# Lookup tables of a state-space layer, built in three portions with a lower place in the order, on VectorE alone

## The chip, the core and the metric

The kernel runs on one core of a Trainium2 chip. The metric is the time of one execution on the device in microseconds (us), lower is better. The engines are called as in the profile: PE is TensorE's matmul, DVE is VectorE, ACT is ScalarE, POOL is GpSimd, SP issues most of the DMAs.

## The reference, cut to what matters

The program is one step of a hybrid encoder over 1072 positions of width 1024: a layer of gated DeltaNet heads (GDN) beside S5 groups, a feed-forward layer (SwiGLU), a layer of forgetting and differential attention, and another feed-forward layer. The change touches only the first. Its S5 part is a diagonal complex state-space model, and the GDN part needs a triangular solve for each block of 64 positions:

```python
def s5_mixer(u, re0, im0, lam_re, lam_im, log_dt, b_re, b_im, c_re, c_im, d_skip, glu_w, glu_b):
    ...
    dt = jnp.exp(log_dt.astype(jnp.float32))[:, None]
    mag = jnp.exp(lr * dt)
    ar, ai = mag * jnp.cos(li * dt), mag * jnp.sin(li * dt)
    ...
    bbr = cr[..., None] * br - ci[..., None] * bi
    bbi = cr[..., None] * bi + ci[..., None] * br
    ...
    _, _, xr, xi = lax.associative_scan(combine, (a_r, a_i, bur, bui), axis=1)
    y = (jnp.einsum('btgp,gmp->btgm', xr, c_re.astype(jnp.float32))
         - jnp.einsum('btgp,gmp->btgm', xi, c_im.astype(jnp.float32))
         + uf * d_skip.astype(jnp.float32).reshape(SSM_GROUPS, SSM_GROUP))

def gated_delta_rule(q, k, v, beta, logg, s0):
    ...
    sol = lax.linalg.triangular_solve(a_low + jnp.eye(CHUNK, dtype=a_low.dtype), rhs,
                                      left_side=True, lower=True)
```

The kernel evaluates the S5 scan by tables that depend on the parameters alone: phases of the powers of the complex pole for 130 steps, and products of the first nine powers with the matrices b and c. These tables are what the change moves.

## The kernel before, in words

Nearly all PE time is dense matmul. The first layer's input projection comes as weight tiles of 128 columns (`dense`): for each tile three chunks of 360, 360 and 352 positions, each of 72 / 3 = 24 matmuls in split precision (`mm3`, L72 to L74). Each chunk fills a PSUM tile `pm`, of which there are two, so PE begins a chunk when the one two before it has been evicted by DVE (L943, a product with the norm `er` into `pre`; 128x360, 128x352 and, for the last chunk split at the group border, 128x32 and 128x328). After the third chunk DVE also makes three convolution steps on the tile (L950, 128x1104) and the low half of the next weights (L38, `wl`).

The 16 tiles of q and k come in three groups of heads (0 to 2, 3 to 5, 6 and 7). After a group's tiles each head has a `pre_head`: decays and products of k and q in PSUM tiles `pk` (L1010, L1011), evicted by DVE (L1014, L1015) into a tile `N`, whose diagonal blocks go to DRAM (L1020, `ndr`). Then `substitute` reads the blocks of the whole group back (L1029, `NB`), inverts them on POOL with 31 pairs of L1037 and L1039, and writes `xdr`. `inverse` then loads the blocks (`iv<-xdr`) and squares its way to the whole inverse on PE, beginning with L1056. Tiles are taken from rings in one pool: `N` and `iv` four each, `ms` and `m2` three each, `gcr` and `TB` two each; a tile's new use waits for the end of its old one. `gcr` is loaded with a head's decays and is last read by POOL's L1017; DVE's first reader of it is L988.

`S5.early` makes the S5 tables. It is a generator: first parameters, then phases (two halves `hh`, table `P`, by doubling, L599 to L609), then for each of four quarters `hf` two complex products with the powers (`ep`, 128x512, and `ca`, 128x576), transposes of `ep` on PE (L631), and a small matmul of `bd` (a `TB` tile) with `ca` (L650) whose result DVE copies out (L652). Every complex product is `cmul` (L406 to L419): four products, one difference, one sum. With `alt=g` two of the four products (L411, L413) run on POOL, the rest on DVE.

The order of instructions on each engine is fixed when the program is built. A scheduler takes instructions by readiness in a model of the engines and, among those, by a priority that follows the order of the code; `next(early)` in the loops over tiles and heads puts the tables' pieces between the pieces of group 0. DMAs of the tables (`s5pd`, `s5ed`, `s5cad`, `hsc`) are issued by SP.

Of the kernel before, what the change touches and what calls it, by code (L numbers as in the profile page):

```python
# [466 lines left out]
SB = {'M': 1, 'D': 4, 'Y': 4, 'ys': 2, 'wU': 2}  # L467
NP = 4


class S5:
# [96 lines left out]
    def early(self, st1, s1t, pkt):  # L568
# [4 lines left out]
        self.params()  # L573
        cc = self.cc
        yield
# [10 lines left out]
        tb = [small("ms", 512, 3) for x in range(3)]  # L586
        cmul(v, bb, [cc[:, x].unsqueeze(2).to_broadcast([128, 16, 16]) for x in range(2)], [mats[:, 0], mats[:, 1]], [m16(x) for x in tb])
        v.tensor_mul(dl, self.dsk.unsqueeze(2).to_broadcast([32, 16, 16]), self.e16.unsqueeze(1).to_broadcast([32, 16, 16]))

        iv = [s1t("iv", 4) for x in range(4)]  # L590
        for hh in range(2):
            ps = slice(8 * hh, 8 * hh + 8)
            P = iv[2 * hh:2 * hh + 2]
            Pv = [x[:, :1088].rearrange("p (a j) -> p a j", a=8) for x in P]
            tv = [x.rearrange("p (a j) -> p a j", a=8) for x in tb]
            v.memset(Pv[0][:, :, 5:6], 1.0)
            v.memset(Pv[1][:, :, 5:6], 0.0)
            for x in range(2):
                v.tensor_copy(Pv[x][:, :, 6:7], self.u8[:, x, ps].unsqueeze(2))  # L599
            n = 1  # L600
            while n < 130:
                m = min(n, 130 - n)
                a = [Pv[x][:, :, 6:6 + m] for x in range(2)]
                b = [Pv[x][:, :, 5 + n:6 + n].to_broadcast([128, 8, m]) for x in range(2)]
                o = [Pv[x][:, :, 6 + n:6 + n + m] for x in range(2)]
                cmul(v, o, a, b, [x[:, :, :m] for x in tv], alt=g if m > 8 else None)
                n += m
                if n == 16:
                    yield  # L609
            for x in range(2):  # L610
                v.tensor_copy(Pv[x][:, :, 0:5], Pv[x][:, :, 5:10])
                for q in range(2):
                    nc.sync.dma_start(self.pd[2 * hh + q, x], P[x][:, 544 * q:544 * q + 544])
            yield
        zero = small("ms", 512, 3)[:16, :112]
        g.memset(zero, 0.0)
        nc.sync.dma_start(self.hsc[:, :, :, 0:112].rearrange("m a e q -> m (a e) q"), zero.unsqueeze(1).to_broadcast([16, 32, 112]))
        t = [iv[0][:, :576], iv[0][:, 576:], iv[1][:, :576]]

        def powers(o, M, ps, nd, neg):  # L620
# [1463 lines left out]
```

## Time and profile before

| | us |
|---|---|
| median of 3 runs | 3350.07 |
| lowest and highest run | 3346.22, 3354.53 |
| the profiled execution | 3354.03 |
| span of its trace | 3352.2 |
| PE busy | 3181.3 (95% of the span) |
| DVE busy | 1909.8 (57%) |
| ACT busy | 1192.7 (36%) |
| POOL busy | 1022.7 (31%) |

The profiled execution took 1.8 us more than its span, and lies 4 us above the median of the runs. Its mean granted clock is 0.969 of full speed. PE is the engine to watch: 3352.2 - 3181.3 = 170.9 us of idle time in all, and where the clock was lower a busy PE does less. The part of the program that the change touches ends about 600 us after the start.

### The profile page before, as it was taken

Reading aid. Unit: us, or ns where it says so; the run is one execution under the profiler, and the core shown is the slowest. Engines: PE = TensorE matmul, PEld = TensorE weight load, DVE = VectorE, ACT = ScalarE, POOL = GpSimd, SP = SyncE. Lnnn points to the kernel's source line nnn. Section 1 sums busy time; section 2 is a strip of 40 time slices with the busy share of each in tenths; the row PEclk is TensorE's granted clock in tenths of the full one; section 3 lists DMA queues with packets and bytes.
Section 4 is the critical chain, followed back from the end, with each engine's and each line's share of the span. In section 5 each row is a group of like instructions: output and inputs, shape, how many; then the busy total and the mean of one; then the engine's idle time right before and its main releaser. Section 6 shows DMA issues by size and latency. Waiting matters only on the chain. (4 is left out here: it accounts for less than half of the span.)

```text
span 3352.2 us, 54659 instructions
## 1 busy us (share of the span) xinstructions
PE 3181.3 (95%) x21673; PEld 3052.7 (91%) x21673; DVE 1909.8 (57%) x3558; ACT 1192.7 (36%) x2221; POOL 1022.7 (31%) x1018
## 2 busy tenths in 40 slices
PE   7899998999989999999999999998998999999997
PEld 6889998998888999999999998876788999999996
DVE  8986554535437655556337225657767655556434
ACT  5434332244434222223114115555655222223112
POOL 2347563412210555541003002223210555551003
PEclk9899999999999999999999999997998999999998
DMA  3454534556432222226113445544424222226211
GB/s 104 157 177 129 167 106 130 160 189 239 162 135 79 77 78 77 78 84 232 52 59 118 162 125 153 158 135 128 139 84 169 77 80 79 78 80 214 74 46 67
DMA packets 167225, 405.24 MB, mean 121 GB/s; under 512 B 42333, under 2 KB 71793, under 8 KB 166969
## 3 DMA queue, kind: packets, MB, share of 16 engines
q1 hardware_dynamic: 142360, 332.86, 31.4%
q10 hardware_dynamic: 16704, 44.33, 3.6%
q0 software_dynamic: 7904, 24.56, 2.1%
q8 instruction: 171, 2.80, 0.3%
q14 instruction: 86, 0.70, 0.1%
HBM read 273.78 MB, written 127.89 MB: 120 GB/s over the span
## 5 line engine op out<-in xcount | busy, mean ns | idle before, releaser
L72 PE MATMUL pm<-mv,wh 128*128 128x352 f32 (+2 forms) x2272 | 752.1, 332 | 28.9 <-DVE pre L943 22.8
L74 PE MATMUL pm<-mv,wl 128*128 128x352 f32 (+2 forms) x2272 | 747.5, 330 | 2.9 <-POOL wl L38 2.3
L73 PE MATMUL pm<-mv,wh 128*128 128x352 f32 (+2 forms) x2272 | 747.9, 329 | 0.0
L72 PEld LDWEIGHTS pm<-mv,wh 128*128 128x128 f32 (+1 forms) x2272 | 429.5, 189 | 38.1 <-issue 15.6
L74 PEld LDWEIGHTS pm<-mv,wl 128*128 128x128 f32 (+1 forms) x2272 | 429.2, 189 | 7.0 <-POOL wl L38 2.9
L73 PEld LDWEIGHTS pm<-mv,wh 128*128 128x128 f32 (+1 forms) x2272 | 429.5, 189 | 3.3 <-issue 0.5
L37 ACT ACTIVATE wh<-wraw 128x512 fp32r<-128x512 f32 (+4 forms) x182 | 148.8, 818 | 702.6 <-PE pm L73 599.6
L255 PE MATMUL pq<-mv,wl 128*128 128x268 f32 x2112 | 295.0, 290 | 8.6 <-DVE xslot L265 3.6
L255 PE MATMUL pq<-mv,wh 128*128 128x268 f32 x2112 | 289.3, 287 | 5.1 <-ACT wh L37 3.2
L255 PEld LDWEIGHTS pq<-mv,wl 128*128 128x128 f32 x2112 | 278.0, 192 | 9.2 <-issue 3.8
L255 PEld LDWEIGHTS pq<-mv,wh 128*128 128x128 f32 x2112 | 272.6, 189 | 6.0 <-ACT wh L37 5.9
L104 POOL TENSOR_TENSOR acc<-acc,sq 128x360 f32<-128x360 f32 (+3 forms) x35 | 35.5, 1013 | 512.1 <-ACT sq L103 511.6
L342 DVE TENSOR_TENSOR xslot<-xslot,pm 128x360 f32<-128x360 f32 x144 | 75.0, 524 | 168.4 <-PE pm L74 168.4
L236 POOL TENSOR_TENSOR sab<-wraw 128x512 f32<-128x512 f32 x20 | 26.2, 1309 | 461.1 <-DMA wraw<-in_w_dram 322.6
L38 DVE TENSOR_TENSOR wl<-wraw,wh 128x512 fp32r<-128x512 f32 (+4 forms) x144 | 135.6, 942 | 45.0 <-ACT wh L37 43.5
L309 POOL TENSOR_TENSOR xslot<-xslot,r 128x1072 f32<-128x1072 f32 x44 | 121.1, 2774 | 0.1
L255 PE MATMUL pq<-us,wl 128*128 128x268 f32 x858 | 119.2, 287 | 0.0
L255 PE MATMUL pq<-us,wh 128*128 128x268 f32 x858 | 118.6, 286 | 0.0
L950 DVE SCALAR_TENSOR_TENSOR cy<-pre,convw,cy 128x1104 f32<-128x1104 f32 x72 | 109.9, 1526 | 14.8 <-ACT cy L948 13.7
L38 DVE TENSOR_TENSOR wh<-sab,wh 128x512 fp32r<-128x512 f32 x88 | 74.3, 846 | 68.2 <-ACT wh L37 68.2
L255 PEld LDWEIGHTS pq<-us,wl 128*128 128x128 f32 x858 | 111.6, 189 | 0.0
L255 PEld LDWEIGHTS pq<-us,wh 128*128 128x128 f32 x858 | 111.0, 188 | 0.0
(765 smaller groups left out, 7073.5 us busy)
## 6 DMA issues: line engine op xcount, KB each, us to landing
ud<-xslot SPq DMA_DIRECT2D x44, 536.0 KB
sab<-ud SPq DMA_DIRECT2D x44, 536.0 KB
wraw<-in_w_dram SPq DMA_DIRECT2D x44, 512.0 KB
xraw<-in_w_dram SPq DMA_DIRECT2D x44, 512.0 KB
wraw<-in_wie_dram SPq DMA_DIRECT2D x36, 512.0 KB
qkvd<-cy ACTq DMA_DIRECT2D x24, 552.0 KB
wraw<-in_wio_dram SPq DMA_DIRECT2D x24, 512.0 KB
kq<-qkvd SPq DMA_DIRECT2D x16, 552.0 KB
```

Source lines behind the costliest of these rows:

```text
L37: nc.scalar.activation(h, src, AF.Copy)
L38: (eng or nc.vector).tensor_sub(l, src, f(h))
L72: nc.tensor.matmul(ps, a, h[:, c0:c1], start=start and k == 0, stop=False)
L73: nc.tensor.matmul(ps, a, l[:, c0:c1], start=False, stop=False)
L74: nc.tensor.matmul(ps, b, h[:, c0:c1], start=False, stop=stop and k == kt - 1)
L104: (eng or nc.gpsimd).tensor_add(acc[:, c0:c1], acc[:, c0:c1], s)
L236: eng.tensor_add(S1, A21, A22)
L255: nc.tensor.matmul(p[:, 512 * j:512 * j + HC], op[:, wo + 128 * k:wo + 128 * k + 128], B[nm][k][:, xo + HC * j:xo + HC * j + HC], start=ne ...
L309: g.tensor_mul(o, o, r)
L342: nc.vector.tensor_add(X[m][:, c0:c1], X[m][:, c0:c1], p)
L950: v.scalar_tensor_tensor(y[:, :TG], pre[:, j:j + TG], convw[:, i, j:j + 1], y[:, :TG], op0=OP.mult, op1=OP.add)
```

## The change

`early` is split. `phasors` (parameters and phases) is written after the `pre_head`s of group 0, and `powers` twice, after those of group 1 (quarters 0 and 1) and of group 2 (quarters 2 and 3). All three stand in `tc.high_priority(offset=-2000)`, which gives their instructions a lower place among those that are ready. `alt=g` is gone from them, so that all six operations of each `cmul` are DVE's. The load of the matrices `mats`, the product `bb` and the term `dl` are made twice, once for each `powers`. In the built program POOL has 27 instructions fewer, DVE 35 more, and PE the same ones in another order.

```diff
+LATER = 2000
...
-    def early(self, st1, s1t, pkt):
+    def phasors(self, st1, s1t):
...
-            P = iv[2 * hh:2 * hh + 2]
+            P = [s1t("iv", 4) for x in range(2)]
...
-                cmul(v, o, a, b, [x[:, :, :m] for x in tv], alt=g if m > 8 else None)
+                cmul(v, o, a, b, [x[:, :, :m] for x in tv])
                 n += m
-                if n == 16:
-                    yield
...
+    def powers(self, st1, s1t, pkt, hfs):
...
+        mats = s1t("N", 4)[:, :1024].rearrange("p (c a b) -> p c a b", c=4, a=16)
+        g.dma_start(mats, I['s5m'])
+        bb = [m16(small("m2", 256, 3)) for x in range(2)]
+        dl = m16(small("m2", 256, 3))[:32]
+        cmul(v, bb, [cc[:, x].unsqueeze(2).to_broadcast([128, 16, 16]) for x in range(2)], [mats[:, 0], mats[:, 1]],
+             [m16(small("ms", 512, 3)) for x in range(3)])
...
-            cmul(v, [f4(x) for x in o], A, B, [f4(x) for x in t], neg_im=neg, alt=g)
-        for hf in range(4):
+            cmul(v, [f4(x) for x in o], A, B, [f4(x) for x in t], neg_im=neg)
+        for hf in hfs:
...
-                N = []
-                for h in range(a, b):
-                    N.append(pre_head(h, nd[h - a]))
-                    next(early, None)
-                    next(early, None)
-                return nd, xd, N
+                return nd, xd, [pre_head(h, nd[h - a]) for h in range(a, b)]
...
                 for h in range(*GR[n]):
-                    for i in (1, 0):
-                        qkv(i, h)
-                        next(early, None)
+                    qkv(1, h)
+                    qkv(0, h)
                 G[n] = group(n)
-                for x in early:
-                    pass
+                with tc.high_priority(offset=-LATER):
+                    if n == 0:
+                        s5.phasors(st1, s1t)
+                    else:
+                        s5.powers(st1, s1t, pkt, (2 * n - 2, 2 * n - 1))
                 group2(n, G[n])
                 group3(n, G[n])
```

The built order shows what this does on the engines (line numbers above 468 are one higher after the change, and 635 to 655 stand for other lines of the tables).

DVE before, inside one dense tile of group 0, some 228 us after the start. The rows with `acc`, `m_744`, `m_745` and `N` are products of the quarters (`N` is here the tile of `mats`, `m_744` and `m_745` are `bb`), between evictions L943 and convolution steps L950:

```order
L943 TENSOR_TENSOR pre<-pm,er 128x360
L950 SCALAR_TENSOR_TENSOR cy<-pre,convw,cy 128x1104
L415 TENSOR_TENSOR iv<-iv 128x512
L414 TENSOR_TENSOR iv<-acc,m_745 128x512
L414 TENSOR_TENSOR iv<-acc,N 128x576
L412 TENSOR_TENSOR iv<-acc,N 128x576
L943 TENSOR_TENSOR pre<-pm,er 128x352
L419 TENSOR_TENSOR iv<-iv 128x512
L38 TENSOR_TENSOR wl<-wraw,wh 128x1024
L415 TENSOR_TENSOR iv<-iv 128x576
L950 SCALAR_TENSOR_TENSOR cy<-pre,convw,cy 128x1104
L417 SCALAR_TENSOR_TENSOR iv<-iv 128x576
```

After the change no such row stands among the tiles of group 0. DVE after, 220 rows later in its order, in the tile that follows the inverses of group 0; the products L411 and L413, which were POOL's, now stand here too:

```order
L944 TENSOR_TENSOR pre<-pm,er 128x352
L419 TENSOR_TENSOR iv<-iv 128x512
L411 TENSOR_TENSOR iv<-acc,N 128x576
L412 TENSOR_TENSOR iv<-acc,N 128x576
L944 TENSOR_TENSOR pre<-pm,er 128x32
L944 TENSOR_TENSOR pre<-pm,er 128x328
L413 TENSOR_TENSOR iv<-acc,N 128x576
L951 SCALAR_TENSOR_TENSOR cy<-pre,convw,cy 128x1104
L414 TENSOR_TENSOR iv<-acc,N 128x576
L415 TENSOR_TENSOR iv<-iv 128x576
L944 TENSOR_TENSOR pre<-pm,er 128x360
```

The quarters 0 and 1 have moved from the tiles of group 0 to the time of its inverses and of the tile after them; quarters 2 and 3 stand in the same way behind the inverses of group 1. The phases stay where they were, among the second to fifth tile.

POOL before, in the middle of the first `substitute`. L1017 is the last reader of the `gcr` of head 2 or 3, and the load of a later head's `gcr` waits for it:

```order
L1039 TENSOR_TENSOR XB<-XB,TB 108x26x6
L1001 COPY egl<-gcr 128x9
L1002 COPY egl<-gcr 128x1
L1037 TENSOR_TENSOR TB<-NB,XB 108x175
L1017 TENSOR_TENSOR gcr<-kq,gcr 128x1104
L1039 TENSOR_TENSOR XB<-XB,TB 108x25x7
```

POOL after, at the beginning of the same `substitute`:

```order
L1018 TENSOR_TENSOR gcr<-kq,gcr 128x1104
L1023 MEMSET N 32x9x32 x4
L1038 TENSOR_TENSOR TB<-NB,XB 108x31
L1040 TENSOR_TENSOR XB<-XB,TB 108x31
L1038 TENSOR_TENSOR TB<-NB,XB 108x60
```

That L1017 (now L1018) has moved ahead of the first step of `substitute`, and no product of the tables is left on POOL around it.

## Rows read from the trace of the kernel before

**Rows 1.** The page, busy time and share of the span, PE alone.

```profile
PE 3181.3 (95%) x21673; PEld 3052.7 (91%) x21673; DVE 1909.8 (57%) x3558; ACT 1192.7 (36%) x2221; POOL 1022.7 (31%) x1018
```

**Rows 2.** Waits of PE, first 900 us: total us, times, longest.

```profile
PE pm L72 <- DVE pre L943: 22.8, 11, 5.1
```

**Rows 3.** Windows of 50 us: PE, PEld, DVE, ACT, POOL busy, granted clock, DMA.

```profile
100.00:150.00 50.00, 39.84 (x232) 38.84 (x232) 48.39 (x150) 26.00 (x27) 21.18 (x33) 0.89 0.35 122
150.00:200.00 50.00, 48.26 (x331) 47.46 (x330) 44.42 (x80) 18.18 (x19) 23.74 (x23) 0.97 0.56 181
200.00:250.00 50.00, 44.84 (x301) 42.82 (x300) 43.95 (x84) 15.59 (x17) 19.25 (x22) 0.97 0.52 167
250.00:300.00 50.00, 44.85 (x273) 43.73 (x272) 33.18 (x71) 23.88 (x24) 41.27 (x63) 0.90 0.38 128
300.00:350.00 50.00, 50.00 (x387) 49.76 (x387) 33.76 (x75) 24.46 (x33) 23.50 (x41) 1.00 0.54 172
350.00:400.00 50.00, 50.00 (x365) 50.00 (x364) 32.01 (x81) 16.36 (x21) 27.50 (x55) 1.00 0.55 174
...
500.00:550.00 50.00, 42.05 (x287) 41.38 (x287) 18.49 (x25) 13.97 (x22) 19.14 (x35) 0.93 0.25 78
```

**Rows 4.** DVE by line and shape, 30 to 420 us: busy us, mean ns.

```profile
L415 DVE TENSOR_TENSOR iv<-iv 128x576 f32<-128x576 f32 x4 | 6.0, 1510 | 4.2 <-PE pk L650 4.2
...
L412 DVE TENSOR_TENSOR iv<-acc,N 128x576 f32<-128x576 f32 x4 | 4.9, 1234 | 0.0
L417 DVE SCALAR_TENSOR_TENSOR iv<-iv 128x576 f32<-128x576 f32 x4 | 4.7, 1174 | 0.0
...
L414 DVE TENSOR_TENSOR iv<-acc,N 128x576 f32<-128x576 f32 x4 | 3.9, 983 | 0.0
...
L412 DVE TENSOR_TENSOR iv<-acc,m 128x512 f32<-128x512 f32 x4 | 2.6, 650 | 0.5 <-DMA s5pd<-iv 0.5
```

**Rows 5.** POOL by line and shape, 30 to 420 us.

```profile
L411 POOL TENSOR_TENSOR iv<-acc,m 128x512 f32<-128x512 f32 x4 | 11.4, 2838 | 12.4 <-DVE iv L415 8.4 <-DMA s5pd<-iv 4.1
```

**Rows 6.** Timeline of DVE: start, us, instruction, wait before it.

```profile
111.72 0.22 DVE L411 TENSOR_TENSOR ms<-iv 128x64 f32<-128x64 f32 x1
...
136.18 1.10 DVE L411 TENSOR_TENSOR ms<-iv 128x64 f32<-128x64 f32 x1
...
278.72 0.51 DVE L988 TENSOR_TENSOR gsm<-gcr,stats 128x9 f32<-128x9 f32 x1 [6.09 <-DMA gcr<-gcd]
```

**Rows 7.** Window of 10 us, columns as in Rows 3.

```profile
280.00:290.00 10.00, 10.00 (x44) 10.00 (x45) 7.24 (x10) 5.15 (x6) 9.48 (x10) 0.55 0.17 54
```

**Rows 8.** Timeline of POOL around the substitutes of groups 0 and 1.

```profile
245.13 0.19 POOL L936 COPY pre<-cstate 128x3 f32<-128x3 f32 x1 [11.43 <-DVE N L1015]
...
259.82 0.24 POOL L1037 TENSOR_TENSOR TB<-NB,XB 108x31 f32<-108x31 f32 x1 [2.96 <-DMA NB<-ndr]
...
268.88 2.56 POOL L1017 TENSOR_TENSOR gcr<-kq,gcr 128x1104 f32<-128x1104 f32 x1
...
311.77 0.25 POOL L1039 TENSOR_TENSOR XB<-XB,TB 108x31 f32<-108x31 f32 x1
374.56 0.24 POOL L1037 TENSOR_TENSOR TB<-NB,XB 108x31 f32<-108x31 f32 x1 [3.51 <-DMA NB<-ndr]
...
419.50 0.25 POOL L1039 TENSOR_TENSOR XB<-XB,TB 108x31 f32<-108x31 f32 x1
```

**Rows 9.** Timeline of PE: a dense stretch, and the first inverse matmul of groups 0, 1, 2.

```profile
317.28 0.32 PE L73 MATMUL pm<-mv,wh 128*128 128x352 f32 x1
317.44 0.32 PE L74 MATMUL pm<-mv,wl 128*128 128x352 f32 x1
...
319.22 0.46 PE L1056 MATMUL gp<-iv,N 128*128 128x128 f32 x2
427.35 0.46 PE L1056 MATMUL gp<-iv,N 128*128 128x128 f32 x2 [1.46 <-DMA iv<-xdr]
523.51 0.77 PE L1056 MATMUL gp<-iv,N 128*128 128x128 f32 x2 [5.61 <-DMA iv<-xdr]
```

More of the change, by code (lines that the diff above doesn't have):

```diff
@@ L566, in params @@
         self.cc = cc
-    def early(self, st1, s1t, pkt):
-        cx, I = self.cx, self.I
-        nc = cx.nc
-        v, g = nc.vector, nc.gpsimd
+    def phasors(self, st1, s1t):
+        nc = self.cx.nc
+        v = nc.vector
         self.params()
-        cc = self.cc
-        yield
-        def small(nm, n, bufs):
-            return st1.tile([128, n], F32, name=nm, bufs=bufs)
-        def m16(x):
-            return x[:, :256].rearrange("p (a b) -> p a b", a=16)
-        mats = s1t("N", 4)[:, :1024].rearrange("p (c a b) -> p c a b", c=4, a=16)
-        g.dma_start(mats, I['s5m'])
-        bb = [m16(small("m2", 256, 3)) for x in range(2)]
-        dl = m16(small("m2", 256, 3))[:32]
[L586 to L590, printed above, removed]
+        tb = [st1.tile([128, 512], F32, name="ms", bufs=3) for x in range(3)]
+        tv = [x.rearrange("p (a j) -> p a j", a=8) for x in tb]
         for hh in range(2):
             ps = slice(8 * hh, 8 * hh + 8)
-            P = iv[2 * hh:2 * hh + 2]
+            P = [s1t("iv", 4) for x in range(2)]
             Pv = [x[:, :1088].rearrange("p (a j) -> p a j", a=8) for x in P]
-            tv = [x.rearrange("p (a j) -> p a j", a=8) for x in tb]
             v.memset(Pv[0][:, :, 5:6], 1.0)
@@ L613, in early, with small, m16, times @@
                     nc.sync.dma_start(self.pd[2 * hh + q, x], P[x][:, 544 * q:544 * q + 544])
[L614 to L617, printed above, removed]
+    def powers(self, st1, s1t, pkt, hfs):
+        cx, I = self.cx, self.I
+        nc = cx.nc
+        v, g = nc.vector, nc.gpsimd
+        cc = self.cc
+        def small(nm, n, bufs):
+            return st1.tile([128, n], F32, name=nm, bufs=bufs)
+        def m16(x):
+            return x[:, :256].rearrange("p (a b) -> p a b", a=16)
+        mats = s1t("N", 4)[:, :1024].rearrange("p (c a b) -> p c a b", c=4, a=16)
[4 more added lines that the diff above has]
+             [m16(small("ms", 512, 3)) for x in range(3)])
+        v.tensor_mul(dl, self.dsk.unsqueeze(2).to_broadcast([32, 16, 16]), self.e16.unsqueeze(1).to_broadcast([32, 16, 16]))
+        if 0 in hfs:
+            zero = small("ms", 512, 3)[:16, :112]
+            g.memset(zero, 0.0)
+            nc.sync.dma_start(self.hsc[:, :, :, 0:112].rearrange("m a e q -> m (a e) q"), zero.unsqueeze(1).to_broadcast([16, 32, 112]))
+        iv = [s1t("iv", 4) for x in range(4)]
         t = [iv[0][:, :576], iv[0][:, 576:], iv[1][:, :576]]
-        def powers(o, M, ps, nd, neg):
+        def times(o, M, ps, nd, neg):
             f4 = lambda x: x[:, :64 * nd].rearrange("p (a d m) -> p a d m", a=4, d=nd)
@@ L623, in powers @@
             B = [M[x][:, ps].unsqueeze(2).to_broadcast([128, 4, nd, 16]) for x in range(2)]
-            cmul(v, [f4(x) for x in o], A, B, [f4(x) for x in t], neg_im=neg, alt=g)
-        for hf in range(4):
+            cmul(v, [f4(x) for x in o], A, B, [f4(x) for x in t], neg_im=neg)
+        for hf in hfs:
             ps = slice(4 * hf, 4 * hf + 4)
             ep = [iv[2][:, :512], iv[2][:, 576:1088]]
-            powers(ep, bb, ps, 8, False)
+            times(ep, bb, ps, 8, False)
             for x in range(2):
@@ L635, in early @@
                 nc.sync.dma_start(self.ed[hf, x], e)
-            yield
             ca = [iv[3][:, :576], iv[3][:, 576:]]
-            powers(ca, [mats[:, 2], mats[:, 3]], ps, 9, True)
+            times(ca, [mats[:, 2], mats[:, 3]], ps, 9, True)
             for x in range(2):
@@ L655, in early @@
                 nc.sync.dma_start(self.hsc[:, ps, e, 112:240], hv[16 * e:16 * e + 16])
-            yield
     def load(self, hf):
```

2 lines of the change are left out of this document (removed).

## The prediction

> **What bounds the kernel now.** The page's busy times come first: PE works for 3181.3 of 3352.2 us [rows 1]. The dense matmuls are all still needed, so the change can only win back time in which PE stands idle or runs at less than the full clock. Next come PE's waits: in the first 900 us the largest entry is the start of a dense chunk that waits for DVE's eviction L943, 22.8 us in eleven waits [rows 2]. DVE as a whole is busy for 57%, but that is a mean; the windows say where it is short. From 100 to 250 us DVE is busy for 48.39, 44.42 and 43.95 of each 50 us, and there PE stands still; from 300 to 400 us PE never stops, and DVE is busy for only 33.76 and 32.01 [rows 3].
>
> I count as lost in a window its idle time and, of its busy time, the share by which the granted clock is below 1. That gives for 100 to 150 us 10.16 + 0.11 x 39.84 = 14.5 us; for 150 to 200 us 1.7 + 1.4 = 3.2; for 200 to 250 us 5.2 + 1.3 = 6.5; for 250 to 300 us 5.15 + 4.5 = 9.6; for 500 to 550 us 7.95 + 2.9 = 10.9 [rows 3]. The clock follows the idle time: after the wait of 5.1 us that ended at 279.8 the next 10 us have PE busy throughout at a granted clock of 0.55, close to the lower level of 1.2 GHz, a loss of another 4.5 us [rows 2, 7]. So a wait costs PE up to twice its length, and a wait saved gives back as much.
>
> **All products on VectorE.** One product of a quarter costs POOL 2.84 us for 128x512 [rows 5]; DVE made a like product, L412 of the same shape, in 0.65 us [rows 4]. Handing DVE six operations in place of four need not make it later. With POOL beside it, the four 128x576 operations of a complex product took 1.23 + 0.98 + 1.51 + 1.17 = 4.9 us [rows 4]. By its width an undisturbed one should take 0.65 x 576 / 512 = 0.73 us, an estimate, so six take 4.4. For 128x512 I charge two more at 0.65, or 1.3. The four quarters thus change by 4 x (1.3 - 0.5) = +3 us; bounds are -2 (no charge for the 128x512) and +6 x 4 (every operation stays at some 1.2 us, the two new ones too). I take +3, because the same DVE operation of 128x64 took 0.22 us with POOL silent and 1.10 us beside POOL's product [rows 6]; the surplus is in the company and not in the shape. The Trainium skill ("SBUF — State Buffer", "Who interferes with whom") says that a VectorE instruction with two inputs in SBUF contends with a GpSimd instruction that reads SBUF. These rows agree, and by it the sum keeps the +3 as long as POOL does not read beside the tables.
>
> The repeated `bb` and `dl` are 7 operations of up to 128x256 at 0.33 us (half of 0.65), 2.3 us on DVE once more. This and the +3 lie in the new places, and are costed there.
>
> **The phases (100 to 160 us).** They stay in the same tiles. DVE gets for each half the two products of 128x128, 128x256 and 128x512, which at 0.65 us for the largest and in proportion are 2 x 1.14 = 2.3 us, 4.6 us for both. It loses the surplus: two rows of 128x64 at about 1.1 us that fall to 0.22, L415 of 128x512 at 1.5 in place of 0.65, and others like them [rows 6], some 5 us. That is nothing, within 2 us. But the first quarter's products, which follow at once, leave these tiles, so that DVE catches up a tile earlier. Of the 14.5 us lost I take 8 as won, the bounds are 0 (DVE is as late as now) and 14.
>
> **The quarters leave group 0 (160 to 300 us).** Here lost time is 3.2 + 6.5 + 9.6 = 19.3 us. All four quarters go from here, at about 8 us of products each (4.9 + 3.1) plus copies, 40 us of DVE's 121 us in 150 to 300. What is left is some 80 of 150 us, as little as in 300 to 400 us, where nothing is lost [rows 3]. The wait of 5.1 us is of another kind: DVE stood for 6.09 us before L988 for the load of `gcr` with the next eviction behind it [rows 6], and that load needed POOL's L1017, which ran only at 268.88, in the middle of `substitute` [rows 8]. In the new order it stands before `substitute`. I take 16 as won, bounds 9 (the `gcr` load or another wait stays) and 19.
>
> **The first inverse.** PE is no longer slowed, but the chain to the inverse is not PE's. In the order after the change, PE's rows between the last product of group 0's heads (L1011) and the first L1056, each at its duration in the trace of before, add up to 55.9 us; in the order of before they are 61.9. The chain beside it: eviction to the reading of the blocks, 245.1 to 259.8 = 14.7 us, `substitute` from 259.8 to 312.0 = 52 us, and 7.2 us to the first inverse matmul at 319.2 [rows 8, 9]. On POOL the second becomes shorter, because the `gcr` product and some evictions' copies are no longer in its midst: its own operations are 41 us, and that of group 1 took 45.2 (374.6 to 419.75) [rows 8]. The table DMAs in front of the block loads leave SP, so the first part is between 8 and 14.7. So the chain is 55 to 68 us, against 55.9: a wait of 0 to 12 us, I take 4, with 2 us more for the clock behind it [rows 7]. Term +6, bounds 0 and +20.
>
> **The quarters beside the inverses.** In 300 to 400 us DVE has 34 us free of 100 [rows 3], and each `powers` brings 2 x (4.4 + 3.9) + 2 x 2 for copies + 2.3 + 1.5 = some 24 us. Over the 81 us of PE work of the inverses and two tiles this fits: 0.66 x 81 + 24 = 78. But it is not spread evenly. Between the evictions of one dense tile (PE about 15 us, 72 matmuls at 0.16 us and small ones [rows 9]) the new order has 19 table rows, 13.5 us at 0.65 to 0.73, beside 0.66 x 15 = 9.9 of other work: 23.4 us of DVE. PE can run two chunks (8 us) ahead of it. Term +3, bounds 0 and +8. Behind group 1 DVE has more free time; nothing.
>
> **Groups 1 and 2.** `substitute` of group 1 and `bd` of the quarters share the two `TB`. Its first step now waits for PE's small matmul of quarter 0; from there to the first inverse matmul PE has 50.4 us, and the chain needs 45.2 or less plus 7.5, 51 to 53, up to 58 if DVE's tables beside it slow POOL. Today's wait is 1.46 us [rows 9]. I take 4 us with 1 us for the clock: term +4, bounds -2 and +12. For group 2 the same count is 58.8 us against about 63; today 5.61 us are waited for and 10.9 lost [rows 3, 9]. Term -2, bounds -10 and +4.
>
> **Sum.** -8 - 16 + 6 + 3 + 4 - 2 = -13 us. The profiled execution of 3354.0 becomes 3341. It lies 4 us above the median of 3350.1, so for a median I say **3337 us**. Later stages change by single rows in their order only, and I give them nothing, with 4 us to either side.
>
> **The rivals.**
> First, *given back*: the waits of the inverses grow as much as the tiles gain. They do so if the chain's part from the heads to the blocks stays 14.7 us and `substitute` stays near 50 us. Then group 0 waits 12 us and loses 5 more at the lower clock, group 1 stands at +8: -24 + 17 + 3 + 8 - 2 = +2, 3352 us. For it speaks that waits of 1.46 and 5.61 us are already there today [rows 9]; against it, that POOL loses all the tables' products. Chance 0.25.
>
> Second, *slower*: the tables' DVE rows delay PE more where they are now than where they were. The place is the tile with 23.4 us of DVE work, and the small matmuls of the quarters in PE's order, which stand in front of dense chunks. It decides if `mats`, which waits for a tile `N` that PE releases only in the second inverse of the group, comes so late that DVE's queue, and with it evictions, stand behind it. With two groups, a stall of 6.1 us as today's for `gcr` [rows 6] in each, and each doubled by the clock, the sum is -13 + 24 = +11 and with tile 15's full 8 us +16: 3366 us. The Trainium skill ("Perfetto Trace Analysis", "Optimizing Scalar/DVE Operations") speaks that way too: it says that with VectorE saturated, moving work to Scalar or even GPSIMD may make sense, and adds that the shared port may keep it from helping. In the phase stage DVE is nearly saturated (48.39 of 50), and the 4.6 us of products would then be a loss [rows 3]. Chance 0.15.
>
> Third, *all won*: neither inverse waits, and nothing is late in the new places: -14 - 19 - 2 = -35, 3315 us. `substitute` would have to follow within 8 us of the heads and run in 41. Chance 0.1.
>
> Fourth, *the phases decide*: the change does not do what it says at its first portion, whose rows stand where they stood. If the 14.5 us of 100 to 150 stay, the sum is -5, 3345 us. Chance 0.1, within the spread of the forecast.
>
> **How the numbers follow.** Forecast 0.4, given back 0.25, slower 0.15, all won 0.1, phases 0.1. A change of 0.3% is 10 us, about what can be told from none: faster is below 3340, slower above 3360. Faster: nearly three quarters of the forecast (0.29), all won (0.1), the part of the phases' case in which the other terms come out better (0.05), and of the first two rivals that in which half of their price stays away (0.09): 0.53. Slower: the second rival and the tail of the first, 0.19. The same: 0.28. The range from 3315 to 3360 leaves out the second rival and a little at the low end.
>
> **What would show it.** Right: the waits L72 <- DVE L943 between 150 and 300 us gone, L988 without a long wait for `gcr`, DVE under 35 of 50 us there, the first inverse matmul well before 319 us, with a wait of 0 to 12 us on its block load, table rows of 128x576 at 0.7 to 0.8 us. Wrong: L411 and L413 on DVE at 1.2 us or more; PE waits of several us for L943 or for the tables' transposes between 300 and 350 us; DVE waiting for `mats`; or the phase stage as slow as it is now.

## The result and the profile after

The changed kernel takes 3374.55 us (median of four runs, 3371.47 to 3380.92); the kernel before, run beside it, 3349.9 (3346.22 to 3354.53). The ratio is 1.0075 [1.0056, 1.0095]: it is slower, by about 25 us. The forecast of 3337 us and its range both missed, and the sign was wrong. The profiled execution took 3380.92 us, 6 us above this median, with a span of 3379.1, 26.9 us more than the span before.

The page's busy times of after, to be read against [rows 1]: PE, the matmuls, has the same count of instructions and is busy 11.8 us longer, and POOL loses 27 us of work. VectorE has 35 instructions more and is busy 4 us less, as its operations became shorter.

```profile
PE 3193.1 (94%) x21673; PEld 3058.2 (91%) x21673; DVE 1905.7 (56%) x3593; ACT 1195.6 (35%) x2221; POOL 996.0 (29%) x991
```

The windows of 50 us, with the columns of [rows 3]:

```profile
100.00:150.00 50.00, 40.37 (x208) 39.10 (x206) 36.13 (x113) 24.85 (x25) 6.42 (x16) 0.80 0.35 113
150.00:200.00 50.00, 49.22 (x333) 49.16 (x333) 33.82 (x83) 19.46 (x19) 6.81 (x19) 0.97 0.44 148
200.00:250.00 50.00, 46.61 (x302) 45.00 (x301) 30.37 (x60) 22.40 (x23) 19.16 (x39) 1.00 0.57 195
250.00:300.00 50.00, 41.90 (x285) 41.70 (x284) 29.60 (x58) 18.44 (x19) 36.10 (x60) 0.90 0.32 95
300.00:350.00 50.00, 46.65 (x373) 45.61 (x372) 36.67 (x109) 18.65 (x33) 13.76 (x25) 1.00 0.64 184
350.00:400.00 50.00, 47.32 (x297) 44.94 (x296) 37.18 (x70) 20.04 (x21) 37.21 (x48) 0.93 0.41 147
...
500.00:550.00 50.00, 45.28 (x274) 43.13 (x273) 23.35 (x29) 13.17 (x12) 47.10 (x69) 1.00 0.23 82
```

Three things stand in them. VectorE has become free where it was short: 36.13, 33.82 and 30.37 us of each 50 between 100 and 250 us, where it had 48.39, 44.42 and 43.95. PE gained next to nothing from it: from 150 to 250 it is busy 2.7 us more, and from 250 to 300 for 41.90 us in place of 44.85. And from 300 to 400 us, where it never stood still before, it now stands 3.35 and 2.68 us, with the clock at 0.93 in the second window.

Lost time, as the prediction counts it, but summed over windows of 10 us, says where the 25 us arise (us lost from the start of the span to the time at the head of the column):

| kernel | 150 | 300 | 450 | 600 | 1000 | 1200 |
|---|---|---|---|---|---|---|
| before | 41.8 | 61.3 | 62.8 | 76.5 | 111.1 | 121.8 |
| after | 44.0 | 60.2 | 74.6 | 91.7 | 130.8 | 140.7 |

Up to 300 us the two are level: nothing was won in the stage whose tiles were to win 24 us. Between 300 and 600 us 16 us are lost more, from there to 1000 some 4 more. The waits of PE in the first 900 us of after (total us, times, longest) name the new places:

```profile
PE gp L1057 <- DMA iv<-xdr: 11.7, 2, 8.7
PE pm L72 <- DVE pre L944: 10.9, 11, 3.1
PE pk L1011 <- DVE N L1016: 10.6, 3, 8.1
PE pm L960 <- ACT pre L956: 8.4, 4, 4.0
PE pm L74 <- POOL wl L38: 4.7, 3, 2.1
```

The waits for the eviction of a dense tile have halved, from 22.8 us [rows 2] to 10.9. In their place have grown the load of the substituted blocks for the inverse (L1057; 7.1 us before), the eviction of a head's matrix (L1016; 2.4 before) and ScalarE's L956, whose result L960 sums (0.3 before).

The wait of 8.1 us has its cause on VectorE. The first two rows are its timeline, the third is PE's:

```profile
286.92 0.27 DVE L645 MEMSET TB<- 128x256 f32 x1 [10.91 <-POOL XB L1040]
287.11 0.23 DVE L1016 SCALAR_TENSOR_TENSOR N<-pk,gsm,N 128x128 f32<-128x128 f32 x1
...
287.39 0.80 PE L1011 MATMUL pk<-kq 128*128 128x128 f32 x2 [8.10 <-DVE N L1016]
```

L645 clears `bd`, the small operand of a quarter. It needs nothing but a free buffer of `TB`, and it stands early in the order, among the evictions of the heads. The buffer is held by the first `substitute` on POOL, which ends at 286.8. So VectorE stands for 10.91 us with the eviction L1016 queued behind the memset, and PE stands behind that.

The same two buffers stop POOL in the other direction, and VectorE once more:

```profile
363.44 3.07 POOL L1038 TENSOR_TENSOR TB<-NB,XB 108x31 f32<-108x31 f32 x1 [10.44 <-PE pk L652]
...
417.89 0.27 DVE L645 MEMSET TB<- 128x256 f32 x1 [9.15 <-POOL XB L1040]
```

The second `substitute` waits for the small matmul L652 of the quarters, and a memset of the next portion for the end of that `substitute`.

The third `substitute` begins at 491.49 us, before at 457.97. Its blocks are not what is late: they are asked for at 456.06, before at 454.69. But its `TB` is held by a quarter of the second portion until that quarter's last L652, and on POOL two products for the weights of dense tiles (L38) stand in front of it in the order. A row of SP, one of PE and two of POOL:

```profile
456.06 0.31 SPq L1030 DMA_DIRECT2D NB<-ndr  x1
...
485.57 1.72 PE L652 MATMUL pk<-iv,TB 128*32 128x128 f32 x14
...
486.71 4.10 POOL L38 TENSOR_TENSOR wl<-wraw,wh 128x1024 fp32r<-128x1024 f32 x1 [6.87 <-ACT wh L37]
...
491.49 0.70 POOL L1038 TENSOR_TENSOR TB<-NB,XB 72x31 f32<-72x31 f32 x1
```

Without a second portion (e13 below) the same `substitute` begins at 461.85, after 2.35 us for its blocks. In after its inverse ends the chain with PE's longest wait here:

```profile
425.27 0.46 PE L1057 MATMUL gp<-iv,N 128*128 128x128 f32 x2 [2.94 <-DMA iv<-xdr]
561.01 0.77 PE L1057 MATMUL gp<-iv,N 128*128 128x128 f32 x2 [8.73 <-DMA iv<-xdr]
```

Against [rows 9] (1.46 and 5.61 us at 427.35 and 523.51) the third group is 37.5 us later.

### The profile page after: what moved, and what is told of

The parts are those of the page before. It is cut to its first block, busy times and chain, and to the rows that moved or that the text cites. A ratio compares the mean times of both kernels' runs of the same rounds, so it can differ in the third digit from the quotient of the medians.

```text
span 3379.1 us, 54664 instructions
## 1 busy us (share of the span) xinstructions
PE 3193.1 (94%) x21673; PEld 3058.2 (91%) x21673; DVE 1905.7 (56%) x3593; ACT 1195.6 (35%) x2221; POOL 996.0 (29%) x991
## 5 line engine op out<-in xcount | busy, mean ns | idle before, releaser
L72 PE MATMUL pm<-mv,wh 128*128 128x352 f32 (+2 forms) x2272 | 752.8, 332 | 17.7 <-DVE pre L944 10.9
L38 DVE TENSOR_TENSOR wl<-wraw,wh 128x512 fp32r<-128x512 f32 (+4 forms) x144 | 134.1, 931 | 41.2 <-ACT wh L37 39.9
L38 DVE TENSOR_TENSOR wh<-sab,wh 128x512 fp32r<-128x512 f32 x88 | 77.2, 878 | 68.0 <-ACT wh L37 68.0
```

The costliest lines, as they stand in the source:

```text
L38: (eng or nc.vector).tensor_sub(l, src, f(h))
L72: nc.tensor.matmul(ps, a, h[:, c0:c1], start=start and k == 0, stop=False)
```

## The experiments

The question to the experiments was which part costs: VectorE alone, the lower place, the shared `TB`, the work of the quarters, or where the portions stand between the groups. Each ratio is to the kernel before, run in the same batch on the same chip; "+7 us" is the ratio less one, times that kernel's 3354 to 3358 us. Every build has its own order on every engine, so one edit also shifts rows far from it. The diffs without another word are against the changed kernel.

### Where it stands, and on which engine

**e1_own_ring**: `bd` gets a buffer of its own; the room comes from `kq` and `gcr`, cut to the width that they use.

```diff
-            bd = small("TB", 256, 2).rearrange("p (x a b) -> p x a b", x=2, a=4)
+            bd = small("bd", 256, 1).rearrange("p (x a b) -> p x a b", x=2, a=4)
...
-                return st1.tile([128, 1152], F32, name=nm, bufs=bufs)
+                return st1.tile([128, TG if nm in ("kq", "gcr") else 1152], F32, name=nm, bufs=bufs)
```

> The changed kernel, but the small tile bd of the quarters has a ring of its own (one buffer) in place of the TB ring that it shares with substitute; so that it fits, the tiles kq and gcr are 1104 columns wide in place of 1152. Theory 1 (the shared ring): the waits of 10.9 and 9.2 us before VectorE's memset of bd, PE's wait of 8.1 us at 287 us with its low clock, and the wait of 10.4 us before the second substitute vanish; 14 to 22 us less than the changed kernel, 3353 to 3360, near the kernel before. Theory 2 (all products on VectorE cost the time) and theory 3 (the place beside the inverses saturates VectorE): within 5 us of the changed kernel, 3370 to 3379.

Measured: 1.0099 [1.0077, 1.0121], +33 us. The wait at L1011 falls to 1.0 us, but the first inverse, at the same time as in after (294.37 against 295.06), now shows the wait itself:

```profile
294.37 0.55 PE L1057 MATMUL gp<-iv,N 128*128 128x128 f32 x1 [8.31 <-DMA iv<-xdr]
```

So the stall at the memset was real and cost nothing of its own up to the first inverse: in its absence PE runs through its work and waits for the same `substitute` 7 us further on. The shared `TB` alone is not the cause.

**e2_pool_back**: the products go back to POOL, in the new places.

```diff
-                cmul(v, o, a, b, [x[:, :, :m] for x in tv])
+                cmul(v, o, a, b, [x[:, :, :m] for x in tv], alt=nc.gpsimd if m > 8 else None)
...
-            cmul(v, [f4(x) for x in o], A, B, [f4(x) for x in t], neg_im=neg)
+            cmul(v, [f4(x) for x in o], A, B, [f4(x) for x in t], neg_im=neg, alt=g)
```

> The changed kernel with two of the four products of each complex product of the tables back on GpSimd (alt=g as before), in the new places. Theory 1: the shared ring still makes VectorE wait, no gain: 3368 to 3390, a surplus on VectorE of 1 us per 128x576 operation beside GpSimd. Theory 2: back near the kernel before, 3350 to 3358.

Measured: 1.0021 [1.0008, 1.0034], +7 us. Its third `substitute` starts at 495.0 and S5's first matmul of the main part stands at 614.7, as late as after's (491.49 and 615.44). From 300 to 600 us it loses 28.5 us, nearly as much as after (31.5; before 15.2). Of the 12 us that its trace has lost less than after's in all, 4 arise up to 300 us and 5 behind 600. So the loss between the groups stays when the products return to POOL, and the 18 us between e2 and after cannot be put down to the engine alone.

**e3_dve_old_place**: the kernel before with VectorE alone, everything in its old place.

```diff
-                cmul(v, o, a, b, [x[:, :, :m] for x in tv], alt=g if m > 8 else None)
+                cmul(v, o, a, b, [x[:, :, :m] for x in tv])
...
-            cmul(v, [f4(x) for x in o], A, B, [f4(x) for x in t], neg_im=neg, alt=g)
+            cmul(v, [f4(x) for x in o], A, B, [f4(x) for x in t], neg_im=neg)
```

> The kernel before with all products of the tables on VectorE, in the old places. Theory 1: as fast as the kernel before or a little faster, 3340 to 3352, since the products that VectorE takes over are paid by the surplus that it loses. Theory 2: as slow as the changed kernel, 3368 to 3380.

Measured: 1.0006 [0.9996, 1.0016], no difference. It has lost 6.5 us less by 300 us (54.8 against 61.3), and gives it back at the first inverse, whose load of the blocks is now waited for:

```profile
325.84 0.77 PE L1056 MATMUL gp<-iv,N 128*128 128x128 f32 x2 [6.32 <-DMA iv<-xdr]
```

**e4_normal_place**: the portions keep their ordinary place in the scheduler's order.

```diff
-LATER = 2000
+LATER = 0
```

> The changed kernel with LATER = 0: the three portions keep their place in the code but no longer have a lower place among ready instructions. Theory 1: the memset of bd still stands before the last evictions of the heads in VectorE's order, so the waits stay: 3368 to 3382. Theory 3 in the form that the lower place delays what PE waits for: 3350 to 3360.

Measured: 1.0063 [1.0043, 1.0083], +21 us. The second `substitute` stands behind L652 for 9.54 us, as in after for 10.44. The lower place alone isn't the cause.

**e7_own_ring_pool_back**: e1 and e2 together (both diffs above).

> The changed kernel with both edits: bd in a ring of its own, and two of four products back on GpSimd. The first two runs gave +30 us for the ring of its own and +9 us for GpSimd's share, against some +24 for the changed kernel. If the two edits act by a mechanism of their own they add up, +10 to +18 us above the kernel before. If it is chance of the order that differs from build to build, anything from +5 to +30.

Measured: 1.0181 [1.0164, 1.0198], +61 us, the worst of all. The main part of S5 begins at 684 us, and 60 us are lost between 600 and 800, with PE's wait for the load of `wT` from the tables (8.84 us) among them (more under e11). Two edits that cost +8 and -18 against after cost +36 together: what a build loses isn't a sum of its edits.

### Without the work

**e5_new_no_quarters** and **e6_old_no_quarters**: the changed kernel, and the one before, with zeros stored in place of the quarters' tables (the phases stay).

```diff
+        flat = s1t("iv", 4)
+        v.memset(flat, 0.0)
...
-            times(ep, bb, ps, 8, False)
...
-                nc.sync.dma_start(self.ed[hf, x], e)
+                nc.sync.dma_start(self.ed[hf, x], flat[:, :512])
+                nc.sync.dma_start(self.cad[hf, x], flat[:, :576])
```

> The changed kernel without the work of the quarters: no products, no transposes and small matmuls, no bd; their tables are stored as zeros by the same DMAs, the phases stay. It bounds what the quarters cost in their new places. Theory P (the quarters beside the inverses hold up PE, by their rows in VectorE's and PE's order and by the shared ring): the whole surplus goes, 15 to 35 us less than the changed kernel, 3340 to 3362. Theory G (the chain of heads, block reading and substitute is the bound and would make PE wait at the first inverses whatever VectorE does): a wait of 6 to 10 us at the first inverse of group 0 stays, lost time until 300 us stays near 60 us, and the kernel is not below the kernel before.

> The kernel before without the work of the quarters, as above: what the quarters cost in their old places among the tiles of group 0. If the prediction's term for these tiles (16 us) were right, 14 to 25 us faster than the kernel before. Theory G: the tiles become faster, but the first inverse matmul then waits 8 us or more for the end of substitute: at most 8 us faster.

Measured: e5 0.9990 [0.9978, 1.0003], e6 0.9982 [0.9970, 0.9994]. This bounds what leaving group 0 can bring, as far as one build can. With all work of the quarters gone from its old place the kernel wins 6 us, of which the two groups of PE's own rows, L650 and L632 (7.9 and 5.0 us of busy time before), would account for more than all. The profiled execution of e6 lies 13 us above its median, so only its rows up to 300 us are read. The first inverse stands at 286.88 us, 32 us earlier than in [rows 9], and waits there:

```profile
286.88 0.58 PE L1020 MATMUL gp<-iv,N 128*128 128x128 f32 x1 [10.01 <-DMA iv<-xdr]
```

From 150 to 300 us VectorE of e6 is busy for 94.67 us in place of 121.55, and PE for 138.60 in place of 137.95. The quarters lay in time in which PE of this build waits for `substitute`.

**e12_skip_quarters_01** and **e13_skip_quarters_23**: the changed kernel with zeros stored for the quarters 0 and 1 alone, or 2 and 3 alone (`blanks` stores them as above; e13 has `n == 2`).

```diff
-                        s5.powers(st1, s1t, pkt, (2 * n - 2, 2 * n - 1))
+                        (s5.blanks if n == 1 else s5.powers)(st1, s1t, pkt, (2 * n - 2, 2 * n - 1))
```

> The changed kernel without the work of quarters 0 and 1 (their tables stored as zeros); quarters 2 and 3 stay. The four quarters cost 27 us together. If the price lies beside group 0's inverses and in the late second substitute: 15 to 25 us less than the changed kernel, +0 to +10 against the kernel before. If it lies behind group 1: 3 to 9 us less, +15 to +22.

> The changed kernel without the work of quarters 2 and 3; quarters 0 and 1 stay. If the price lies beside group 0's inverses: +15 to +22 against the kernel before. If it lies behind group 1 (the third substitute starts at 491 us in place of 458, then PE waits 8.7 us for its blocks): +0 to +10. If each quarter costs its share, both runs are at +9 to +12.

Measured: e12 0.9979 [0.9966, 0.9992], -7 us; e13 1.0003 [0.9993, 1.0012], +1 us. Against e5, with neither (-3), the first portion adds 4 us and the second takes 4 off, which is no more than the intervals; both add 28. The quarters that are left out take some 6 us of PE's own rows with them in each of the two. Neither portion costs much by itself. With one of them missing the third `substitute` begins at 468.1 (e12) or 461.9 (e13), with both at 491.49.

**e14_no_matmuls** and **e15_no_products**: the changed kernel with half the work of its quarters. e14 leaves out PE's transposes and small matmuls, e15 the products on VectorE; the tables hold other numbers in both.

```diff
-            hp = pkt()
-            for a in range(4):
-                for x in range(2):
-                    nc.tensor.matmul(hp[:32, a * 128:(a + 1) * 128], bd[:, x, a], ca[x][:, a * 144:a * 144 + 128], start=x == 0, stop=x == 1)
```

```diff
-            times(ep, bb, ps, 8, False)
...
-            times(ca, [mats[:, 2], mats[:, 3]], ps, 9, True)
```

> The changed kernel without the quarters' transposes and small matmuls on PE: ep is stored untransposed, and hv is copied from ca; all of VectorE's rows stay, bd too. The 96 matmuls take some 14 us of PE themselves. If PE's own rows are the price, with the waits that they make in PE's order: -15 to -25 us against the changed kernel, +0 to +10. If it is VectorE's rows that hold up evictions: -5 to -14 only.

> The changed kernel without the quarters' sixteen halves of complex products on VectorE (ep and ca are zeros set once), with all of PE's rows, bd and the stores. 48 operations of 0.68 to 0.74 us, 34 us of VectorE, are gone. If VectorE's rows are the price: -13 to -25 us against the changed kernel, +0 to +12. If PE's rows and the shared ring are: within 8 us of the changed kernel, +16 to +28.

Measured: e14 1.0113 [1.0087, 1.0139], +38 us; e15 1.0107 [1.0090, 1.0124], +36 us. With less work both are slower than after (+25). Both are outside what was expected. In e14 the order has a new stall: on VectorE an eviction waits for the store `usc<-cy` to read out its buffer, and PE waits behind it (a row of VectorE, then one of PE):

```profile
403.74 0.85 DVE L881 TENSOR_TENSOR cy<-pm,er 128x32 f32<-128x32 f32 x2 [18.25 <-DMA usc<-cy]
...
404.74 0.63 PE L72 MATMUL pm<-mv,wh 128*128 128x352 f32 x1 [11.46 <-DVE gsm L952]
```

e15 has lost only 60.7 us by 600 us, 16 less than the kernel before, and then 68 between 600 and 800, where S5's main part waits for its tables. PE's waits of e15 in that stretch begin:

```profile
PE pk L739 <- DMA wT<-hsc: 12.7, 2, 8.8
PE pk L741 <- DVE sD L415: 11.6, 3, 5.5
PE pm L72 <- ACT gh L37: 10.8, 2, 8.2
```

So the amount of work on PE or on VectorE is not by itself what costs. What costs is who stands behind whom, and it can be anywhere up to 800 us.

### The chain of substitute

**e8_after_half_substitute** and **e9_before_half_substitute**: every second step of `substitute` is left out, in the changed kernel and in the one before.

```diff
-                for j in range(31):
+                for j in range(0, 31, 2):
```

> The changed kernel with every second of the 31 steps of substitute left out (16 stay). It shortens the chain on GpSimd from the heads to the first inverse matmul, and nothing else. Theory G (that chain is the bound of this part): the first inverse moves ahead by some 20 us, the waits for the blocks (2.9 and 8.7 us) and the waits of VectorE's memset for the shared ring (10.9 and 9.2 us) shrink to under 3 us each, 15 to 25 us less than the changed kernel, 3350 to 3360. Theory P (tables' rows beside the inverses hold up PE): within 8 us of the changed kernel.

> The kernel before with every second step of substitute left out, the control to the run above. Before, PE waits for the blocks for 1.5 and 5.6 us only, with some 4 us more for the clock. Theory G: 5 to 12 us faster than the kernel before. Theory P: the same, so that it is the difference to the run above that tells.

Measured: e8 1.0052 [1.0034, 1.0069], +17 us; e9 1.0007 [0.9997, 1.0016], +2 us. Halving the chain on POOL takes 8 of 25 us off the change and nothing off the kernel before. In the latter the waits move: a dense tile waits 6.31 us for an eviction that stands on VectorE behind 10.23 us for `gcr`, and the second inverse waits 8.06.

```profile
279.84 0.64 PE L72 MATMUL pm<-mv,wh 128*128 128x360 f32 x1 [6.31 <-DVE pre L943]
...
395.88 0.77 PE L1056 MATMUL gp<-iv,N 128*128 128x128 f32 x2 [8.06 <-DMA iv<-xdr]
```

By this pair its length explains a third.

**e10_before_substitute_dve** and **e11_after_substitute_dve**: the steps of `substitute` go from POOL to VectorE, in the kernel before and in the changed one.

```diff
-                    g.tensor_mul(t, nbv[:, j, j + 1:32].unsqueeze(2).to_broadcast([n, m, j + 1]),
+                    v.tensor_mul(t, nbv[:, j, j + 1:32].unsqueeze(2).to_broadcast([n, m, j + 1]),
...
-                    g.tensor_sub(xbv[:, j + 1:32, 0:j + 1], xbv[:, j + 1:32, 0:j + 1], t)
+                    v.tensor_sub(xbv[:, j + 1:32, 0:j + 1], xbv[:, j + 1:32, 0:j + 1], t)
```

> The kernel before with the products and differences of substitute on VectorE in place of GpSimd. Theory G: the chain becomes shorter (an operation of 250 elements takes some 0.4 us on VectorE against 0.6 on GpSimd, and no other work of GpSimd stands between), but VectorE, which is short of time until 260 us, gets some 20 us more for each group: between -10 and +15 us.

> The changed kernel with substitute on VectorE. There VectorE has 20 of 50 us free while the first substitute runs. Theory G: the wait for the shared ring cannot block any more, since both sides are in one engine's order, the first inverse moves ahead: 10 to 30 us less than the changed kernel, 3345 to 3365. Theory P: the tables' rows and substitute's compete on VectorE beside the inverses, 3370 or more.

Measured: e10 0.9963 [0.9951, 0.9974], -12 us; e11 1.0105 [1.0090, 1.0120], +35 us. In e10 none of the three inverses waits, and the third comes at 504.23 us, 19 us earlier than in [rows 9]. In e11 the loss comes between 600 and 800 us (65 us), with waits of PE for the loads of `wT` (9.67 us) and `sca` (3.65). There the table of the last quarter comes late. Its store (L657), and the first load of the matrices by S5's main part (L667), of e11 and then of e7:

```profile
629.57 0.79 SPq L657 DMA_DIRECT2D hsc<-iv  x2
...
636.70 0.91 SPq L667 DMA_DIRECT2D sca<-s5cad  x2
...
666.15 0.80 SPq L657 DMA_DIRECT2D hsc<-iv  x2
...
669.19 1.43 SPq L667 DMA_DIRECT2D sca<-s5cad  x2
```

In after the two stand at 544.85 and 598.98. In e7 the operands of that quarter's small matmuls were ready at 537 us, and the matmuls stand in PE's order at 659.9 to 664.9, behind the dense tiles that follow. In e15 the store is late too (614.45), but the load comes 30 us behind it, after the stores of the third group's inverses. So the second portion has two ways to cost: it holds up the third `substitute`, or it is itself too late for S5's main part.

### Other places

**e16_all_quarters_after_group1**: all four quarters in one portion, behind group 1.

```diff
-                    else:
-                        s5.powers(st1, s1t, pkt, (2 * n - 2, 2 * n - 1))
+                    elif n == 1:
+                        s5.powers(st1, s1t, pkt, (0, 1, 2, 3))
```

> The changed kernel with all four quarters in one portion after the heads of group 1, none after group 2. The mats load, bb and dl are made once. If the link is the second portion standing between group 2's heads and the third substitute: the third substitute starts before 470 us, S5's main part before 595 us, -5 to +12 us against the kernel before. If the quarters beside the inverses of group 0 hold up everything behind them: second substitute later than 375 us, +20 us or more.

Measured: 1.0008 [0.9998, 1.0018], as before. The time is as expected and the way to it isn't: the third `substitute` begins at 507 us and the main part at 622, later than after's, while I had them earlier. But PE's waits at the second and third inverse are 3.77 and 3.75 us, and 300 to 600 us loses 20.8 us, against 31.5 in after and 15.2 in before. Three windows of 150 us, first of after, then of e16 (columns as in [rows 3]):

```profile
150.00:300.00 150.00, 137.73 (x916) 135.86 (x916) 93.78 (x198) 60.31 (x59) 62.07 (x117) 0.95 0.44 146
300.00:450.00 150.00, 139.97 (x998) 135.68 (x997) 97.60 (x236) 51.24 (x73) 80.03 (x119) 0.97 0.51 158
450.00:600.00 150.00, 136.09 (x900) 132.54 (x899) 81.28 (x127) 39.95 (x53) 79.02 (x105) 0.97 0.29 97
```

```profile
150.00:300.00 150.00, 138.04 (x909) 136.26 (x910) 93.61 (x197) 60.84 (x60) 62.65 (x120) 0.94 0.43 144
300.00:450.00 150.00, 143.52 (x995) 138.88 (x994) 106.15 (x243) 47.40 (x62) 73.98 (x105) 0.99 0.50 159
450.00:600.00 150.00, 140.03 (x966) 138.44 (x965) 71.97 (x112) 47.20 (x67) 78.86 (x121) 0.98 0.29 97
```

The same work in one portion costs nothing that can be told from no change (`mats`, `bb` and `dl` are made once here); in two, with a group between them, it costs 25 in after. The first memset still waits in e16 (10.82 us), as in after, so that stall is again not the price.

**e17_old_place_dve_substitute_dve**: e3 and e10 together, against the kernel before: products and substitutes on VectorE, all in the old places. **e18_substitute_12_dve**: the kernel before with only the substitutes of groups 1 and 2 on VectorE.

```diff
-                substitute(nd, xd, 36 * (b - a))
+                substitute(nd, xd, 36 * (b - a), v if n else g)
```

> The kernel before with all products of the tables and substitute on VectorE, GpSimd without either. With substitute alone on VectorE it was 12 us faster than the kernel before, with the products alone on VectorE +3 us (no difference). If both add up: -6 to -14 us.

> The kernel before with the substitutes of groups 1 and 2 on VectorE and that of group 0 left on GpSimd. VectorE is short of time until 260 us and free from 300 us on. If the gain of the run with all three on VectorE comes from the waits of 1.5 and 5.6 us for the blocks of groups 1 and 2: -10 to -16 us, as much as or more than with all three.

Measured: e17 0.9952 [0.9936, 0.9968], -16 us, the fastest of all; e18 0.9985 [0.9975, 0.9995], -5 us. Two windows of e17 show that a busy VectorE need not slow PE:

```profile
150.00:200.00 50.00, 49.63 (x347) 48.86 (x346) 43.60 (x84) 18.59 (x19) 7.90 (x17) 1.00 0.60 195
...
400.00:450.00 50.00, 47.67 (x323) 46.74 (x322) 42.94 (x89) 15.41 (x19) 17.33 (x22) 1.00 0.32 96
```

By 600 us it has lost 54.0 us in place of 76.5, by 1200 us 101.9 in place of 121.8: the win arises early and stays. VectorE is busy for 43.60 us here as it was before (44.42), but POOL beside it for 7.90 in place of 23.74. The expectation of e18 failed: -5 in place of -10 to -16, so the gain of e10 does not come from the waits for the blocks of groups 1 and 2 alone.

Set side by side, the builds fall in two groups. The nine with quarters in both new portions (after, e1, e2, e4, e7, e8, e11, e14, e15) lie at +7 to +61 us against the kernel before, the four with one such portion or none (e5, e12, e13, e16) at -7 to +3. From 300 to 600 us the latter lose 20 to 26 us; of the nine, six lose 28 to 47, e8 with its halved `substitute` 23, and e11 and e15, which lose only 9 and 2 there, lose 65 and 68 between 600 and 800. So that two portions cost is not the chance of one build, but how much is.

## Why the prediction was wrong

Three terms of the sum failed: the phases, the tiles of group 0 with the first inverse, and the links between the groups. They are some 11, 7 and 11 us off; most of what is left of the miss lies behind 600 us, to which the sum gave nothing.

**The price of the products was right.** In after, VectorE's rows by shape between 30 and 520 us read (busy us, mean ns):

```profile
L411 DVE TENSOR_TENSOR iv<-acc,N 128x576 f32<-128x576 f32 x4 | 4.8, 1188 | 0.0
...
L412 DVE TENSOR_TENSOR iv<-acc,N 128x576 f32<-128x576 f32 x4 | 3.0, 745 | 0.0
L417 DVE SCALAR_TENSOR_TENSOR iv<-iv 128x576 f32<-128x576 f32 x4 | 3.0, 744 | 0.0
```

745 and 744 ns where 0.73 us was estimated and 1234 and 1174 ns stood before [rows 4]. The mean of 1188 is made of three rows near 0.74 us and one of 2.52 at 488.90, which runs beside POOL's product L38 of 128x1024 (486.71 to 490.81). L413 has one such row, 2.51 us at 475.64, beside the L38 before it (473.53 to 477.53). The surplus is indeed in the company. The Trainium skill ("SBUF — State Buffer", "Who interferes with whom") puts contention between VectorE and GpSimd down to a port pair that they share. These rows agree as far as they go: they show the contention, not the port. By e3 all this is worth nothing in time (1.0006).

**The quarters leave group 0, and the first inverse: -16 + 6 us predicted, -3 measured** (16.2 us lost from 150 to 300, in before 19.5; the first inverse of after lies in that stretch). The relief came: VectorE is under 35 of 50 us, and the waits for the eviction of dense tiles fell in this stretch from 7.9 to 3.1 us. `gcr` was not part of it: VectorE still waits for it, three times and 9.8 us in all, 4.60 the longest, where it was once 6.09 [rows 6]. But I added to the relief a separate term for the first inverse, +6, as if that chain began later and were slightly longer than PE's work. The two are one balance. PE's work up to the inverse and `substitute` beside it end at nearly the same time; what PE gains in the tiles it waits for at the inverse, 8.31 us in e1, 6.32 in e3, 10.01 in e6. e6 bounds the gain, with no quarters at all anywhere: 6 us. The first rival, *given back*, has this right, with a wait of 12 us at the first inverse and 5 more at the lower clock; after has 8.10 us at L1011, and in the 10 us from 287 to 297 a granted clock of 0.71.

**The phases: -8 us predicted, +3 measured** (17.7 us lost from 100 to 150, before 14.5). Here too VectorE got free (36.13 us), and something else is last. PE's waits for L943, 10.0 us in this window before, are down to 1.6, and PE waits for ScalarE's L956 three times, 8.1 us. Two of them:

```profile
106.32 1.01 PE L960 MATMUL pm<-ones,pre 128*128 128x1 f32 x4 [3.98 <-ACT pre L956]
...
128.69 0.48 PE L960 MATMUL pm<-ones,pre 128*128 128x1 f32 x3 [3.39 <-ACT pre L956]
```

I had put all of the 14.5 us down to VectorE because it was the busy engine. That it would be ScalarE's order next, where L998 and L1001 of the heads stand in front of L956 (103.08 to 105.2 us), wasn't in the bounds; the fourth rival (*the phases decide*) comes nearest, with the 14.5 us as they were.

**The links between groups: +4 - 2 + 3 predicted, +16 measured from 300 to 600 us.** I saw one of them, POOL's step behind PE's small matmul, and charged 4 us. POOL stood for 10.44, and VectorE stood for the memsets behind `substitute` 10.91 and 9.15 us; that direction I had not looked at, though the same two buffers make it. The second rival, *slower*, foresaw VectorE's queue behind one waiting instruction with the evictions behind it, twice; it named `mats` as the place, where the wait is short (1.59 us), so that its price of 3366 us, 9 below the result, is near by luck in part. That it takes both portions is shown by e12, e13 and e16 against the nine builds that have both. That it isn't the buffer alone, the lower place alone or the amount of work, by e1, e4, e14 and e15; that it isn't the engine alone, by e3 in the old places and by the loss from 300 to 600 us that stays in e2. How the second portion holds up the third group in after is shown by the rows at 456 to 491 us; that this is the whole of the 16 us is not shown.

**What stays open.** Which row of the order turns the links into 25 us in this build and 7 in e2 was not settled. Removing a wait moved it (e1, e9), and every build has another order, so part of the 25 us may be an unlucky arrangement of rows that no part of the change contains. The cause of the +4 us between 600 and 1200 stays open. Between 2000 and 2800 after loses 5 us more (94 against 89), but there all the builds lie between 86 and 103, though no edit touches that part.

## What to carry to other kernels

Before you count relief on a busy engine as time won, look for the next chain that the waiting engine meets: leave the work out altogether once and see what that brings, which here was 6 us where 16 less 6 were forecast. A buffer shared by work on two engines is a wait in both directions, and a clearing that needs only the buffer may be placed far ahead in an in-order queue, with urgent work behind it. And when a chain on a slow engine is what is waited for, try to move the chain: in the kernel before, `substitute` on VectorE brought 12 us, and 16 with the products there too, while moving the tables out of its way brought none. It is no rule, as the same move in the changed kernel left it at +35.

## What the runs showed that was not expected

In the kernel before, VectorE does the steps of `substitute` beside its own work without losing time: e10 takes 1973.7 us of VectorE in place of 1909.8 and 119.5 us less of POOL (903.2 against 1022.7), and PE's busy time falls from 3181.3 to 3173.5. Less work can make a build slower: e14 and e15 leave out half of the quarters and are 11 to 13 us behind the change, with stalls such as the 18.25 us at L881 where none was, or a table that comes too late. And effects of single edits do not add: two portions that alone change +4 and -4 us cost 28 together, and e7 costs 61 us where its parts cost 33 and 7.
